# A two-layer hybrid trunk on one core: the whole body placed in a block whose instruction order comes from another scheduler model

## The chip, the cores and the metric

The kernel runs on one core of a Trainium2 chip. The time is that of the device, in microseconds (us), from the launch of the program to its end; the median of several runs is compared. The core has five engines that run their own instruction streams in order and wait for each other by semaphores: PE (TensorE, matmuls; its weight loads are shown as PEld), DVE (VectorE), ACT (ScalarE), POOL (GpSimd) and SP (SyncE, which here issues the DMAs of the weights).

## What is computed

The reference is a decoder trunk of two residual layers over 512 tokens of width 1024, float32:

```python
for i in range(DEPTH):                       # DEPTH = 2
    h = rms_norm(x, mix_norm[i])
    if i % 2 == 0:                           # layer 0
        x = x + concat([ssd_mixer(...), gla_mixer(...)]) @ w_out    # parts of h @ w_in
    else:                                    # layer 1
        x = x + mla(h)                       # latent attention, 16 heads, causal
    f = rms_norm(x, ffn_norm[i])
    x = x + (silu(f @ w_gate[i]) * (f @ w_up[i])) @ w_down[i]       # 2816 hidden
```

The SSD mixer has a causal convolution of width 4, SiLU, a chunked scan over 128 tokens, a gate `silu(z)` and an RMS norm over two groups of 512 features. The GLA mixer is a gated linear attention in chunks of 64 tokens. The attention has low-rank q and kv with norms, a rotary part and per-head norms of q and k.

## The kernel before

The residual lies feature-major in eight tiles of 128 features x 512 tokens. Every dense product runs in float32 accuracy out of three matmuls: weight and activation are each split into two parts, `hi` and `lo` (names `whi`/`wlo`, `xh`/`xl`, `mxh`/`mxl`, `fhh`/`fhl`), and `mm3` (L140 to L143) adds `hi*hi`, `lo*hi` and `hi*lo` in one PSUM bank. `weight` (L125 to L138) loads one piece of a weight, mostly 128 x 1024: a DMA on SP's queue into `wraw` (2 buffers), a cast on ACT to `whi` (L135) and a subtraction on DVE to `wlo` (L136), 3 buffers each. One such piece feeds 24 matmuls of 128 x 512. The next weight's steps are written with a raised priority (`AHEAD`, 90), so the scheduler puts them before work that the program has earlier.

Accumulators (`acc`) share three PSUM banks in turn: the fourth needs the bank of the first, so it waits for whatever reads that one. The other banks belong to roles (`st`, `a1`, `a2` in layer 0; `sco`, `ptr`, `po` in the attention).

Norms (`rstd`, L165 to L178): ones-matmuls sum the squares into `st` (L168), DVE takes the reciprocal root by a bit estimate and three Newton steps on a 128x128 tile, 12 small instructions (`rs_m`, `rsi`, `rsy`, `rst`, L156 to L161), four matmuls with `sel` spread it (L175) and ACT copies it to `R` or `Rg` (L177). The factor `R` is applied late, when a product of the layer is read out of PSUM: `xpad` (L320, input of the convolution, whose taps are `cva`, L322 and L325), `fg` and `fu` (L634, L637, gate and up of the FFN), `zh`, `kr`, `qd`. So the first products of a stage need `R` only when their bank has to come free.

Stages: the mixer with its convolution, SSD groups g = 0 and 1 (their outputs `y`, normed by `Rg` at L426, split to `mxh`, `mxl`, and taken into the residual by `out_round`), four GLA heads with three more rounds; the FFN, 22 pairs of gate and up and then the down products; the attention: low-rank products (`lh`, `ll`, squares `lsq`, per-token factors `lry`), `project` per group of four heads (q to `qs` through `acc`, k and v to `ks` and `v`, evicted with the factor `lry`; per-head sums `st` by reduces at L799 to L802, roots `hry`, then `qs` and `ks` scaled, L807 to L814, and rotated, L732 to L735), `prepare` (transposes of `ks` and `qs` to `kT` and `qT`, L821 to L836, through `acc`) and `attend` (L848 to L867); a second FFN. The number behind a name here and below is that of the buffer.

What sets the order: the program text gives instructions priorities in the order written (weights raised), and a scheduler at compile time orders each engine's stream by these priorities and by a model of when each instruction could run. The streams are then fixed; on the chip each engine takes its next instruction and waits if that isn't ready.

Of the kernel before, what the change touches and what calls it, by code (L numbers as in the profile page):

```python
# [15 lines left out]
DRAM = bass.MemoryType.DRAM  # L16
# [15 lines left out]
# columns of the packed per-partition vectors  # L32
# [11 lines left out]

@with_exitstack
def kernel(ctx: ExitStack, tc: tile.TileContext, A, yT, stop=99):
# [20 lines left out]
    def open_phase(**tags):  # L67
        """the other banks, by role"""
        if phase:
            phase["pool"].__exit__(None, None, None)  # L70
        phase["pool"] = tc.tile_pool(name=nm("pph"), bufs=1, space=PSUM)
        phase["p"] = phase["pool"].__enter__()
        phase["tags"] = tags
# [26 lines left out]
    # sel[:, c]: row 32 c is one  # L100
# [4 lines left out]
    # tri[s, l] = 1 where s <= l  # L105
# [10 lines left out]
    def split(raw_ap, th, tl, bufs, pool):  # L116
        """raw float32 [128, 512] -> exact parts hi + lo, both float32r"""
        hi = pool.tile([P, T], F32R, tag=th, name=nm(th), bufs=bufs)
        lo = pool.tile([P, T], F32R, tag=tl, name=nm(tl), bufs=bufs)
        S.copy(hi, raw_ap)  # L120
        V.tensor_tensor(lo, raw_ap, hi.bitcast(F32), ALU.subtract)
        return hi, lo

    def weight(src, kc, m):
        """src: DRAM AP [128, kc, m]; loaded and split ahead of what comes before it here"""  # L125
        with tc.high_priority(offset=AHEAD):
            return weight_now(src, kc, m)
# [17 lines left out]
    def dense(ps, w, xs):  # L145
        """ps[m, t] = sum over the chunks of w (stationary) and xs [(hi, lo)]"""
        n = len(xs)
        for k, (xh, xl) in enumerate(xs):
            mm3(ps, w[0][:, k, :], w[1][:, k, :], xh, xl, k == 0, k == n - 1)

    def rsqrt(pool, m, shape, tag, ytag=""):
        """1/sqrt(m) by bit estimate and three Newton steps; m > 0"""
        h = pool.tile(shape, I32, tag=tag + "i", name=nm(tag + "i"), bufs=1)
        y = pool.tile(shape, F32, tag=tag + ytag + "y", name=nm(tag + "y"), bufs=1)
        t = pool.tile(shape, F32, tag=tag + "t", name=nm(tag + "t"), bufs=1)
        V.tensor_scalar(h, m.bitcast(I32), 1, None, ALU.logical_shift_right)  # L156
        V.tensor_scalar(y.bitcast(I32), h, -1.0, float(0x5F3759DF), ALU.mult, ALU.add)
        for _ in range(3):
            V.tensor_tensor(t, y, y, ALU.mult)
            V.scalar_tensor_tensor(t, m, -0.5, t, ALU.mult, ALU.mult)  # L160
            V.scalar_tensor_tensor(y, t, 1.5, y, ALU.add, ALU.mult)  # L161
        return y

    def rstd(ssq, n, pool, tag):
        """ssq [128, 512]: partial sums of squares -> R [128, 512], 1/rms on every partition"""  # L165
        ps = aux()
        for c in range(4):
            E.matmul(ps[32 * c:32 * c + 32, :P], ones, ssq[:, c * P:(c + 1) * P],  # L168
                     start=True, stop=True)
        m = const.tile([P, P], F32, tag="rs_m", name=nm("rs_m"))  # L170
        V.tensor_scalar(m, ps[:, :P], 1.0 / n, EPS, ALU.mult, ALU.add)
        y = rsqrt(const, m, [P, P], "rs")
        pb = aux()
        for c in range(4):
            E.matmul(pb[:, c * P:(c + 1) * P], sel[:, c, :], y, start=True, stop=True)  # L175
        R = pool.tile([P, T], F32, tag=tag, name=nm(tag), bufs=1)
        S.copy(R, pb)  # L177
        return R  # L178

    class Norm:  # L180
        """collects the chunks of the residual: squares, and x * gain in two parts"""
# [26 lines left out]
    def tok_scalar(R):  # L208
        """R [128, 512] with equal rows -> [128 tokens, 4]"""
        ps = aux()  # L210
        for c in range(4):
            E.transpose(ps[:, c * P:(c + 1) * P], R[:, c * P:(c + 1) * P], ident)
        r = const.tile([P, 4], F32, tag="rtok", name=nm("rtok"))
        V.tensor_copy(r, ps.rearrange("p (c x) -> p c x", c=4)[:, :, 0])
        return r

    def gate(pool, tag, ps, R, bufs):
        """silu(ps * R)"""
        h = pool.tile([P, T], F32, tag="cva", name=nm(tag + "h"), bufs=2)
        V.scalar_tensor_tensor(h, ps, 0.5, R, ALU.mult, ALU.mult)  # L220
        t = pool.tile([P, T], F32, tag="cvt", name=nm(tag + "t"), bufs=2)
        S.activation(t, h, AF.Tanh)
        g = pool.tile([P, T], F32, tag=tag, name=nm(tag), bufs=bufs)
        V.scalar_tensor_tensor(g, t, 1.0, h, ALU.add, ALU.mult)
        return g

# [8 lines left out]
    def out_round(r, parts, nxt=None):  # L235
        """residual += (4 chunks of the mixed width) @ their rows of w_out"""
        for m2 in range(4):
            w = weight(A["w_out"][r, m2], 4, 256)
            for j in range(2):
                m = 2 * m2 + j  # L240
                ps = acc()
                dense(ps, (w[0][:, :, j * P:(j + 1) * P], w[1][:, :, j * P:(j + 1) * P]), parts)
                V.tensor_tensor(X[m], X[m], ps, ALU.add)
                if nxt is not None:
                    nxt.add(m)
# [8 lines left out]
    with tc.tile_pool(name="gkp", bufs=1) as gkp:  # L254
        rtok = tok_scalar(R)
        # dt (rows 0..15) and the low-rank gate input (rows 32..47)
# [9 lines left out]
        # dt = softplus(dt_raw + bias), token-major [128, chunk, head]  # L266
# [41 lines left out]
        with tc.tile_pool(name="ssd", bufs=2) as sp:  # L308
# [4 lines left out]
            def conv(i, tag, bufs, bank=acc):  # L313
                """silu(causal conv) of chunk i of x|B|C, feature-major"""
# [18 lines left out]
            def group(g):  # L333
                """B and C of a group: cb[s, l] for s <= l, C feature-major, B token-major"""
# [23 lines left out]
            def core(f, xs, zg, cb, cT, btok):  # L358
                """the scan of two heads, gated by silu(z)"""
# [8 lines left out]
                # decay times cb, [s, head, chunk, l]  # L368
# [8 lines left out]
                # exp(a_cum) on the features' partitions  # L377
# [3 lines left out]
                # x * dt, token-major; and that times the decay to the chunk's end  # L381
# [10 lines left out]
                # states at the chunk starts  # L392
# [39 lines left out]
            def values(h):  # L432
                """v of a GLA head, token-major"""
# [36 lines left out]
        with tc.tile_pool(name="gla", bufs=2) as gp:  # L470
# [5 lines left out]
            # log-sigmoid of the gates, summed inside chunks of 64  # L476
# [19 lines left out]
            def inner(h, after_dense=None):  # L496
                """normalised head output times its gain; two chunks of 128 values"""
# [3 lines left out]
                # exp(g_last / 16) of each chunk  # L501
# [12 lines left out]
                # queries of a pair's second chunk, decayed from the pair's start  # L514
# [29 lines left out]
                # scores, transposed: [key, pair, query]  # L544
# [12 lines left out]
                # keys at the pairs' ends, token-major, and the states  # L557
# [109 lines left out]
    with tc.tile_pool(name="mla", bufs=2) as mp, tc.tile_pool(name="mla1", bufs=1) as m1:  # L667
        r1 = tok_scalar(R)
        # tables with the gains: rope(x) = x * ra + swapped x * rb, for q and for k
# [12 lines left out]
        # causal mask: zeros, then -1e30 where key > query in the last block  # L682
# [5 lines left out]
        # rotary key, feature-major raw  # L688
# [5 lines left out]
        # low-rank q and kv: raw (without 1/rms of the residual), times their gains, in two parts;  # L694
        # per-token factors: cf = r1 / rms(r1 * raw)
# [29 lines left out]
        # rotary key: token-major norm and rotation, back to feature-major  # L725
        def rope(dst, src, tab, shape):
            """dst = src * ra + swapped src * rb; shape [128, 4, heads, 32]"""
# [40 lines left out]
        def project(g):  # L768
            """q, k (normalised, rotated) and v of four heads, token-major"""
            # q of four heads  # L770
# [11 lines left out]
            # k and v of four heads  # L782
# [12 lines left out]
            # 1/rms per head  # L795
# [21 lines left out]
        def prepare(g, hp, qs, ks, v):  # L817
            """keys and queries of two heads, feature-major"""
# [21 lines left out]
        def attend(g, hp, v, kts, qts):  # L840
            """two heads: scores, softmax, values"""
            po = aux("po")
            for b in range(4):
                n = (b + 1) * P
                pts = []
                for j in range(2):
# [4 lines left out]
                    # -scale * (scores + mask), and its minimum  # L851
# [6 lines left out]
                    # probabilities, transposed: [key, key block, query]  # L858
# [13 lines left out]
        def o_round(r, nxt=None):  # L872
            """residual += half of the heads @ their rows of w_o"""
# [31 lines left out]
def _layout(inp):  # L905
# [5 lines left out]
    def pieces(w, kc, m):  # L911
        """[K, M] -> [M / m, 128, kc, m]"""
# [10 lines left out]
    # [head, half of the chunks, 128, 4 chunks, 256]  # L923
    a["w_v"] = np.ascontiguousarray(v.reshape(2, 4, P, 4, 256).transpose(3, 0, 2, 1, 4))
    a["w_g"] = pieces(g, KD, P)
    # [round of 4 chunks, pair of column chunks, 128, 4, 256]
# [7 lines left out]
    # [group of 4 heads, 128, 3, 384]  # L934
    a["w_uq"] = pieces(i["w_uq"][0], 3, 384)
    # [group, 128, 2, (k | v) x 4 heads x 64]
# [22 lines left out]
    # rotary tables, of shapes alone: [128, (cos | sin with sign), 4, 32]  # L959
# [26 lines left out]
```

## Time and profile before

| | us |
|---|---|
| median of 3 runs (lowest, highest) | 1395.1 (1395.07, 1395.79) |
| span of the profiled execution | 1393.5 |
| PE busy | 1373.1 (99%) |
| DVE busy | 786.1 (56%) |
| ACT busy | 559.6 (40%) |

The profile has one execution of the kernel. Its span goes from the first to the last recorded instruction, and lies 1.6 us under the median of the timed runs. A row of the timeline has start and duration in us, engine, line of the kernel, operation, output and inputs; in square brackets the idle time ahead of it and what ended that. A row of a stretch (`0.00:50.00`) has its length, then for each engine the busy time and in brackets the number of instructions, the clock granted to TensorE (1.00 is full), and the use of the DMAs. A row of waits has who waited for whom, the total, how often, and the longest. A row of groups has line, engine, operation, the tiles with their shape, count, then busy time and the mean of one in ns, then the idle time of the engine just before them and what ended it. Matmul records overlap: one of 128 x 512 is shown for 0.39 us, and the next starts 0.23 us after it.

### The profile page before, as it was taken

The numbers are of one execution on the slowest core, as the hardware profiler recorded it, in microseconds if no ns is written. First come the engines' busy times: TensorE is split into PE (matmuls) and PEld (weight loads), VectorE is DVE, ScalarE is ACT, GpSimd is POOL, SyncE is SP. The second block draws the span as 40 slices with busy tenths as digits, with TensorE's granted clock in tenths as the row PEclk, the third lists the DMA queues.
The fourth block names the chain that finished last, engine by engine and source line by source line (L and its number), as shares of the span: only waits on it lengthen the run. The fifth ranks groups of instructions, "written<-read, shape, count | busy, mean of one in ns | idle before, by whom it ended". The sixth has DMA issues, their size and how long they took to land.

```text
span 1393.5 us, 17395 instructions
## 1 busy us (share of the span) xinstructions
PE 1373.1 (99%) x6842; PEld 1108.1 (80%) x6842; DVE 786.1 (56%) x1407; ACT 559.6 (40%) x934; POOL 9.1 (1%) x40
## 2 busy tenths in 40 slices
PE   7999999999999999999999998999999999999998
PEld 5798888687788888888888787767688888888887
DVE  7877956767667444444333459776684444443221
ACT  5665623544334232232232247774753323232111
POOL 0000000000000000000000000000000000000000
PEclk9999999999999999999999999999999999999999
DMA  5343232212233333333333321102023333333331
GB/s 174 108 148 94 68 99 77 65 57 76 65 102 91 93 104 92 105 91 94 92 101 96 99 68 49 44 31 76 1 76 106 91 103 93 92 105 102 105 109 64
DMA packets 36722, 122.21 MB, mean 88 GB/s; under 512 B 4737, under 2 KB 5761, under 8 KB 36641
## 3 DMA queue, kind: packets, MB, share of 16 engines
q1 hardware_dynamic: 35600, 120.70, 28.7%
q8 instruction: 54, 0.88, 0.3%
q10 hardware_dynamic: 1040, 0.41, 0.1%
q14 instruction: 28, 0.22, 0.1%
HBM read 118.96 MB, written 2.13 MB: 87 GB/s over the span
## 4 chain that ended last, share of the span: by engine, by line
PE 94%; DVE 4%; DMA 1%; issue 1%; ACT 1%; SPq 0%; DVEq 0%; ACTq 0%
PE acc L142 27%; PE acc L143 27%; PE acc L141 27%; PE sco L848 3%; PE po L867 2%; PE ptr L861 2%; PE st L175 1%; PE a L409 1%; DVE wlo L136 1%; PE a L579 1%; PE a L395 0%; DMA acb<-acd 0%; PE a L581 0%; PE a L413 0%; PE a L142 0%
## 5 line engine op out<-in xcount | busy, mean ns | idle before, releaser
L135 ACT CAST whi<-wraw 128x1024 fp32r<-128x1024 f32 (+2 forms) x223 | 226.6, 1017 | 576.8 <-PE acc L142 519.5
L143 PE MATMUL acc<-xh,wlo 128*128 128x512 f32 (+1 forms) x1152 | 452.5, 393 | 0.0
L142 PE MATMUL acc<-xl,whi 128*128 128x512 f32 (+1 forms) x1152 | 451.9, 392 | 0.0
L141 PE MATMUL acc<-xh,whi 128*128 128x512 f32 (+1 forms) x1152 | 451.0, 392 | 0.0
L136 DVE TENSOR_TENSOR wlo<-wraw,whi 128x1024 fp32r<-128x1024 f32 (+2 forms) x223 | 263.0, 1180 | 177.0 <-ACT whi L135 176.1
L142 PEld LDWEIGHTS acc<-xl,whi 128*128 128x128 f32 (+1 forms) x1152 | 215.7, 187 | 47.3 <-issue 3.1
L143 PEld LDWEIGHTS acc<-xh,wlo 128*128 128x128 f32 (+1 forms) x1152 | 215.7, 187 | 45.8 <-issue 1.8
L141 PEld LDWEIGHTS acc<-xh,whi 128*128 128x128 f32 (+1 forms) x1152 | 215.8, 187 | 45.1 <-issue 1.1
L141 PE MATMUL acc<-fhh,whi 128*128 128x512 f32 x288 | 112.0, 389 | 0.0
L142 PE MATMUL acc<-fhl,whi 128*128 128x512 f32 x288 | 112.0, 389 | 0.0
L143 PE MATMUL acc<-fhh,wlo 128*128 128x512 f32 x288 | 112.0, 389 | 0.0
L637 DVE TENSOR_TENSOR fu<-acc,R 128x512 f32<-128x512 f32 x44 | 30.4, 691 | 139.4 <-PE acc L143 139.4
L634 DVE TENSOR_TENSOR fg<-acc,R 128x512 f32<-128x512 f32 x44 | 30.4, 691 | 95.2 <-PE acc L143 91.3
L142 PEld LDWEIGHTS acc<-fhl,whi 128*128 128x128 f32 x288 | 54.1, 188 | 11.3
L143 PEld LDWEIGHTS acc<-fhh,wlo 128*128 128x128 f32 x288 | 54.1, 188 | 11.2
L141 PEld LDWEIGHTS acc<-fhh,whi 128*128 128x128 f32 x288 | 54.1, 188 | 11.1
L141 PE MATMUL acc<-mxh,whi 128*128 128x512 f32 x128 | 50.4, 396 | 1.3 <-ACT whi L135 1.3
L142 PE MATMUL acc<-mxl,whi 128*128 128x512 f32 x128 | 50.4, 395 | 0.0
L143 PE MATMUL acc<-mxh,wlo 128*128 128x512 f32 x128 | 50.3, 394 | 0.0
L848 PE MATMUL sco<-kT,qT 96*128 96x128 f32 (+3 forms) x128 | 45.4, 448 | 0.9 <-DVE mx L852 0.7
L852 DVE CUSTOM_DVE_ANT_0 sc<-sco,am 128x128 f32<-128x128 f32 (+3 forms) x64 | 30.8, 485 | 13.0 <-PE sco L848 12.4
L854 ACT ACTIVATE sc<-sc,mx 128x128 f32<-128x128 f32 (+3 forms) x64 | 35.8, 561 | 3.8 <-DVE mx L852 2.8
(290 smaller groups left out, 1590.6 us busy)
## 6 DMA issues: line engine op xcount, KB each, us to landing
wraw<-in_w_gate_dram SPq DMA_DIRECT2D x44, 512.0 KB, 3.6
wraw<-in_w_up_dram SPq DMA_DIRECT2D x44, 512.0 KB, 3.6
wraw<-in_w_down_dram SPq DMA_DIRECT2D x32, 512.0 KB, 3.6
wraw<-in_w_out_dram SPq DMA_DIRECT2D x16, 512.0 KB, 3.7
wraw<-in_w_xbc_dram SPq DMA_DIRECT2D x12, 512.0 KB, 3.7
wraw<-in_w_down_dram SPq DMA_DIRECT2D x16, 384.0 KB, 3.1
wraw<-in_w_z_dram SPq DMA_DIRECT2D x8, 512.0 KB, 3.6
wraw<-in_w_v_dram SPq DMA_DIRECT2D x8, 512.0 KB, 3.7
```

What stands on the lines that cost most here:

```text
L135: S.copy(hi[:, :kc * m], r)
L136: V.tensor_tensor(lo[:, :kc * m], r, hi.bitcast(F32)[:, :kc * m], ALU.subtract)
L141: E.matmul(out, ah, bh, start=first, stop=False)
L142: E.matmul(out, ah, bl, start=False, stop=False)
L143: E.matmul(out, al, bh, start=False, stop=last)
L634: V.tensor_tensor(g, pg, R, ALU.mult)
L637: V.tensor_tensor(u, pu, R, ALU.mult)
L848: E.matmul(ps[:, :n], qts[j][:, b * P:(b + 1) * P], kts[j][:, :n], start=True, stop=True)
L852: V.tensor_tensor_reduce(sc[:, :n], ps[:, :n], am[:, T - n:], -scale, 3e38, ALU.add, ALU.min, mx[:, 0:1])
L854: S.activation(sc[:, :n], sc[:, :n], AF.Exp, bias=mx[:, 0:1], scale=-1.0, accum_out=mx[:, 1:2])
L861: E.transpose(ps[:, kb * P:(kb + 1) * P], sc[:, kb * P:(kb + 1) * P], ident)
L867: E.matmul(po[64 * j:64 * j + 64, b * P:(b + 1) * P], v[:, kb, 2 * hp + j, :], pts[j][:, kb * P:(kb + 1) * P], start=(kb == 0), stop=(kb = ...
```

## The change

The body, until now `tile_trunk_kernel`, becomes a function `trunk`, and `tile_trunk_kernel` opens a block on the tile context around its call. The block is ordered with a timeline model of the engines in place of the scheduler's usual one. No operation, tile, buffer count or priority changes; comments and docstrings go, and lines in the body move down by 5.

```diff
+def tile_trunk_kernel(tc: tile.TileContext, A, yT):
+    with tc.block(name="trunk", schedule_with_timeline_sim=True):
+        trunk(tc, A, yT)
+
+
 @with_exitstack
-def tile_trunk_kernel(ctx: ExitStack, tc: tile.TileContext, A, yT, stop=99):
+def trunk(ctx: ExitStack, tc: tile.TileContext, A, yT, stop=99):
     nc = tc.nc
     V, S, G, E = nc.vector, nc.scalar, nc.gpsimd, nc.tensor
```

All five streams hold the same instructions in another order. Of PE's 6288, 3558 stand at the same place, of DVE's 1409, 454, of ACT's 880, 342, of SP's 250, 231, of POOL's 45, 31. In both FFNs the order is the same apart from their first 20 us; the mixer, the attention and the joints between stages differ.

DVE near the start, the instructions up to `xpad_66`, which takes the accumulator `acc_65` out of its bank (`cva` are the taps of the convolution, `dr`, `db`, `dp` the small chain of the time step, `bT` the activated B). Before:

```order
L280 TENSOR_TENSOR db_255<-da_252 128x64
L330 SCALAR_TENSOR_TENSOR bT_49_338<-cvt_48_336,cva_47_331 128x512
L282 TENSOR_SCALAR dp_260<-db_255 128x64
L325 SCALAR_TENSOR_TENSOR cva_55_374<-xpad_54_371,cw_295,cva_55_374 128x512
L284 SCALAR_TENSOR_TENSOR dp_260<-dp_260,db_255 128x64
L320 TENSOR_TENSOR xpad_66_427<-acc_65_402,R_32_193 128x512
```

And now:

```order
L219 COPY rtok_34_207<-st_33_202 128x4
L330 SCALAR_TENSOR_TENSOR cva_47_332<-xpad_46_329,cw_296,cva_47_332 128x512
L330 SCALAR_TENSOR_TENSOR cva_55_375<-xpad_54_372,cw_296,cva_55_375 128x512
L141 TENSOR_TENSOR wlo_130_726<-wraw_128_723,whi_129_725 128x1024
L276 TENSOR_TENSOR dr_251<-st_39_246,dtb_242 128x64
L325 TENSOR_TENSOR xpad_66_428<-acc_65_403,R_32_194 128x512
L325 TENSOR_TENSOR xpad_95_569<-acc_94_544,R_32_194 128x512
```

The weight part `wlo_130` now stands ahead of `xpad_66`, right behind the last taps of `cva_47` and `cva_55`; of the small chain of the time step, which was mixed in with the taps, only `dr` is still ahead of it. The weight part `wlo_122`, which came after `xpad_66`, stands just above these rows, ahead of `dg`.

PE at the norm of the second SSD group (`st_384` spreads the root; `acc_428` is the first product of the `out_round` behind it, with the normed `y` as `mxh` and `mxl`). Before:

```order
L142 MATMUL acc_403_2303<-wlo_399_2221,xh_14_139 128x256
L175 MATMUL st_384_2185<-rsy_382_2172,sel_97 128x128 x4
L143 MATMUL acc_403_2303<-whi_398_2220,xl_15_140 128x256
L141 MATMUL acc_403_2303<-whi_398_2220,xh_17_146 128x256
L142 MATMUL acc_403_2303<-wlo_399_2221,xh_17_146 128x256
L143 MATMUL acc_403_2303<-whi_398_2220,xl_18_147 128x256
```

And now:

```order
L147 MATMUL acc_419_2415<-xl_24_162,whi_417_2411 128x512
L148 MATMUL acc_419_2415<-xh_23_161,wlo_418_2412 128x512
L180 MATMUL st_384_2186<-rsy_382_2173,sel_98 128x128 x4
L146 MATMUL acc_428_2459<-mxh_386_2194,whi_426_2455 128x512
L147 MATMUL acc_428_2459<-mxl_387_2195,whi_426_2455 128x512
L148 MATMUL acc_428_2459<-mxh_386_2194,wlo_427_2456 128x512
L146 MATMUL acc_428_2459<-mxh_388_2199,whi_426_2455 128x512
```

Before, `st_384` stood within `acc_403`, and 60 rows of other matmuls lay between it and `acc_428`; now it stands behind the whole of `acc_419`, and `acc_428` follows it at once.

DVE at the start of the attention, from the scaling of `ks_1171` to the last step of the rotation of `qs_1157`, which PE then transposes (`st_1205` and `sq_1204` belong to the second group of heads, `qs_1157` to the first). Before:

```order
L814 TENSOR_TENSOR ks_1171_6670<-ks_1171_6670,hry_1180_6719 128x1024
L732 TENSOR_TENSOR rt_1183_6735<-rr_1182_6733,csq_6271 128x16x16
L733 TENSOR_TENSOR rt_1183_6735<-rr_1182_6733,csq_6271 128x16x16
L734 TENSOR_TENSOR qs_1157_6607<-rr_1182_6733,csq_6271 128x16x32
L799 TENSOR_REDUCE st_1205_6843<-sq_1204_6842 128x16
L735 TENSOR_TENSOR qs_1157_6607<-qs_1157_6607,rt_1183_6735 128x16x32
L800 TENSOR_REDUCE st_1205_6843<-sq_1204_6842 128x16
```

And now:

```order
L819 TENSOR_TENSOR ks_1171_6671<-ks_1171_6671,hry_1180_6720 128x1024
L804 TENSOR_REDUCE st_1205_6844<-sq_1204_6843 128x16
L805 TENSOR_REDUCE st_1205_6844<-sq_1204_6843 128x16
L737 TENSOR_TENSOR rt_1183_6736<-rr_1182_6734,csq_6272 128x16x16
L738 TENSOR_TENSOR rt_1183_6736<-rr_1182_6734,csq_6272 128x16x16
L739 TENSOR_TENSOR qs_1157_6608<-rr_1182_6734,csq_6272 128x16x32
L809 TENSOR_SCALAR st_1205_6844<-st_1205_6844 128x16
L141 TENSOR_TENSOR wlo_1277_7111<-wraw_1275_7108,whi_1276_7110 128x1024
L809 TENSOR_SCALAR st_1205_6844<-st_1205_6844 128x16
L835 TENSOR_SCALAR kT1_6598<-acc_1211_6876,pv_89 64x512
L807 TENSOR_REDUCE st_1205_6844<-sq_1204_6843 128x16
L740 TENSOR_TENSOR qs_1157_6608<-qs_1157_6608,rt_1183_6736 128x16x32
```

The reduce of 512 columns, the weight part `wlo_1277`, the copy `kT1` and the third reduce now stand ahead of the last step of `qs_1157`; so do `wlo_1267` and `wlo_1270`, which stood behind it before and are now further up among the roots `hry_1180`.

More of the change, by code (lines that the diff above doesn't have):

```diff
@@ L42, with kernel @@
 NPV = _n
+def kernel(tc: tile.TileContext, A, yT):
+    with tc.block(name="trunk", schedule_with_timeline_sim=True):
+        trunk(tc, A, yT)
 @with_exitstack
-def kernel(ctx: ExitStack, tc: tile.TileContext, A, yT, stop=99):
+def trunk(ctx: ExitStack, tc: tile.TileContext, A, yT, stop=99):
     nc = tc.nc
```

## The prediction

> **What bounds the kernel now.** I read the page first: how busy each engine is, and the chain that ended last.
>
> ```profile
> span 1393.5 us, 17395 instructions
> PE 1373.1 (99%) x6842; PEld 1108.1 (80%) x6842; DVE 786.1 (56%) x1407; ACT 559.6 (40%) x934; POOL 9.1 (1%) x40
> PE 94%; DVE 4%; DMA 1%; issue 1%; ACT 1%; SPq 0%; DVEq 0%; ACTq 0%
> ```
>
> TensorE (PE) is the bound, and an order without any operation added or removed can change the time only by making PE stand still more or less. So the second view is busy time by stretches: 0 to 435 us is the mixer, 435 to 800 the first FFN, 800 to 1025 the attention, the rest the second FFN.
>
> ```profile
> core 0: us, PE busy (x) PEld busy (x) DVE busy (x) ACT busy (x) POOL busy (x), PEclk, DMA share, GB/s
> 0.00:50.00 50.00, 42.41 (x198) 30.84 (x199) 38.77 (x76) 25.34 (x39) 3.20 (x22) 1.00 0.39 133
> 250.00:300.00 50.00, 46.89 (x259) 36.82 (x257) 35.02 (x58) 22.89 (x35) 0.00 (x0) 0.97 0.22 64
> 450.00:500.00 50.00, 50.00 (x222) 41.42 (x221) 23.48 (x29) 15.12 (x19) 0.00 (x0) 1.00 0.34 98
> 850.00:900.00 50.00, 46.26 (x278) 34.03 (x276) 41.66 (x129) 37.80 (x87) 0.00 (x0) 1.00 0.14 44
> 900.00:950.00 50.00, 49.15 (x296) 32.06 (x295) 36.87 (x125) 36.37 (x93) 0.00 (x0) 1.00 0.14 43
> ```
>
> In an FFN (450 to 500) PE never idles: 222 matmuls in 50 us, one each 0.225 us. PE stands still 7 us at the start, 3 us in 250 to 300, and 3.7 us in 850 to 900, where DVE is busy 83% of the time. The third view, PE's waits, names them:
>
> ```profile
> PE a L141 <- ACT xh L193: 6.9, 1, 6.9
> PE a L548 <- DVE ki L529: 1.6, 1, 1.6
> PE acc L834 <- DVE qs L735: 1.4, 1, 1.4
> PE acc L141 <- ACT whi L135: 1.3, 1, 1.3
> PE acc L834 <- DVE kT L830: 1.0, 1, 1.0
> PE acc L821 <- ACT qT L836: 0.7, 2, 0.6
> ```
>
> The first is the load of the input, which no order moves. So what the old order visibly loses is about 8 us. A new order has little to win that shows, and every place where it lets PE run into an unfinished result is a loss. A dense matmul's record lasts 0.39 us while the next starts 0.225 us later, so waits under 0.165 us at hand-overs stay hidden; there are some 200 hand-overs between dense and small matmuls in mixer and attention, so at most 33 us could hide there.
>
> **The change part by part.** Nothing is added or removed; instructions of each engine change places. Both FFN bodies keep their order. SP's queue keeps 231 of 250 places, and a weight lands 3.6 us after its issue (row below) against a weight's 5.4 us of matmuls (24 of 0.225); I cost it at nothing. The terms are the places where PE now meets a result just made, worked out with the durations of these groups:
>
> ```profile
> L135 ACT CAST whi<-wraw 128x1024 fp32r<-128x1024 f32 x197 | 207.0, 1051 | 516.2 <-PE acc L142 468.3 <-issue 33.8 <-PE acc L143 7.8
> L136 DVE TENSOR_TENSOR wlo<-wraw,whi 128x1024 fp32r<-128x1024 f32 x197 | 240.6, 1222 | 171.0 <-ACT whi L135 170.1 <-PE st L168 0.7
> L325 DVE SCALAR_TENSOR_TENSOR cva<-xpad,cw,cva 128x512 f32<-128x512 f32 x36 | 26.7, 742 | 0.2
> L320 DVE TENSOR_TENSOR xpad<-acc,R 128x512 f32<-128x512 f32 x10 | 6.9, 686 | 0.5 <-PE acc L143 0.5
> L634 DVE TENSOR_TENSOR fg<-acc,R 128x512 f32<-128x512 f32 x44 | 30.4, 691 | 95.2 <-PE acc L143 91.3 <-ACT R L177 3.9
> L799 DVE TENSOR_REDUCE st<-sq 128x16 f32<-128x1024 f32 x4 | 4.9, 1214 | 2.5 <-ACT sq L798 2.5
> wraw<-in_w_gate_dram SPq DMA_DIRECT2D x44, 512.0 KB, 3.6
> 229.47 0.59 ACT L177 COPY Rg<-st 128x512 f32<-128x512 f32 x1 [0.45 <-PE st L175]
> ```
>
> *T1, the start.* `acc_102` is the fourth user of three accumulator banks: it must wait for `xpad_66`, which reads `acc_65`. The new DVE order puts much ahead of `xpad_66`. Counting from the start of `st_31`: ACT casts `whi_121` first (1.05), then copies R (1.64); DVE does `wlo_122` (2.3), `dg` and two `xpad` (4.4), six `cva` (8.9), `rtok`, `wlo_130` (10.3), `dr` (10.6), `xpad_66` (11.3). PE has until then only `st_31` (0.9), 24 matmuls of `acc_94` (5.4) and eight small ones (0.8): it stands from 7.1 to 11.3, **+4.2**.
>
> *T2, norm of the second SSD group, then `out_round`.* The rows of before for the same chain:
>
> ```profile
> 228.30 1.13 PE L175 MATMUL st<-rsy,sel 128*128 128x128 f32 x8 [0.18 <-DVE rsy L161]
> 230.19 2.73 DVE L426 SCALAR_TENSOR_TENSOR y<-y,pv,Rg 128x512 f32<-128x512 f32 x4
> 231.97 2.18 ACT L120 CAST mxh<-y 128x512 fp32r<-128x512 f32 x4
> 232.84 1.89 DVE L121 TENSOR_TENSOR mxl<-y,mxh 128x512 fp32r<-128x512 f32 x3
> 243.92 0.39 PE L141 MATMUL acc<-mxh,whi 128*128 128x512 f32 x1
> ```
>
> From `st` to the first `mxl` written are 5.2 us (228.30 to 232.84, and 0.68 for one), and PE came for it only at 243.92: hidden. In the new order the dense matmuls stand right behind `st_384`, with `whi_436` and `wlo_437` in the chain: 1.05 + 0.59 + 0.6 (the rest of `wlo`) + 2.73 + 0.7 = 5.7, less 1.1 of PE's own work, **+4.6**.
>
> *T3, both FFN starts.* `acc_743` waits for `fg_732`, as `acc_727` holds its bank. New order: from `st_722` on ACT casts `whi_753` (1.05) ahead of R, DVE does `wlo_754` (to 2.3) ahead of `fg` (3.0); PE has 0.9 of work: 2.1 each, **+4.2**.
>
> *T4, attention start.* Three places. (a) `acc_1176` needs the bank of `acc_1173`, whose eviction needs `lry_1149`. In before that chain took 4.3 us:
>
> ```profile
> 829.23 0.16 DVE L718 SCALAR_TENSOR_TENSOR lm<-sco,rtok 128x4 f32<-128x4 f32 x1 [1.21 <-PE sco L716]
> 833.34 0.15 DVE L722 TENSOR_TENSOR lry<-lry,rtok 128x4 f32<-128x4 f32 x1
> 850.84 0.68 DVE L735 TENSOR_TENSOR qs<-qs,rt 128x512 f32<-128x512 f32 x1
> 851.44 0.68 DVE L800 TENSOR_REDUCE st<-sq 128x16 f32<-128x512 f32 x1
> 851.67 1.05 PE L834 MATMUL acc<-ident,qs 128*96 128x128 f32 x8 [1.41 <-DVE qs L735]
> 854.77 0.75 DVE L830 TENSOR_SCALAR kT<-acc,pv 64x512 f32<-64x512 f32 x1
> ```
>
> Now two reduces (1.21 + 0.68) stand in it and it begins later: some 6.1, plus two evictions 0.7, less 2.7 of matmuls: 4.1. (b) Ahead of the last `qs` that `acc_1212` transposes there are now two more `wlo` (128x768 and 128x384, together 1.4 by their share of the 1.22 of a full one), a reduce of 0.68, a `wlo` of 1.22, `kT` 0.75 and a reduce of 1.21: 5.3 more than in before, where PE already waited 1.4: 6.7. (c) `acc_1271` waits for the bank of `acc_1216`, read by `kT3`, which stands behind the next group's rsqrt and three scalings: 2.8. Together 13.6, less what this stretch waited before (1.4 + 1.0 + 0.7), **+10.5**.
>
> *T5, the clock.* A long stop costs twice. Before, after the 1.62 and 1.29 us near 264, matmuls started 0.43 apart for 3.2 us:
>
> ```profile
> 262.00:264.00 2.00, 0.94 (x5) 0.44 (x3) 2.00 (x4) 0.06 (x1) 0.00 (x0) 1.00 0.02 8
> 264.00:266.00 2.00, 0.34 (x4) 0.20 (x4) 2.00 (x5) 1.80 (x3) 0.00 (x0) 0.92 0.02 4
> 266.00:268.00 2.00, 1.81 (x4) 1.49 (x5) 2.00 (x5) 0.76 (x3) 0.00 (x0) 0.50 0.04 8
> 268.00:270.00 2.00, 2.00 (x8) 1.60 (x7) 1.32 (x2) 0.81 (x2) 0.00 (x0) 0.72 0.00 0
> ```
>
> At a granted 0.50 that is 1.6 us lost. I count it after T1, T2 and once in T4, **+4.8**. The Trainium skill ("TensorE: Matmul & The Clock Gate", section "HAM oscillation — how this bites in real kernels") says to leave PE no idle gap over about 3.4 us, as the clock then falls to half for a window; by it T4 would pay twice and the sum would be 1.6 higher. The trace agrees that a stretch with little PE work is followed by about 3.2 us at half clock.
>
> *Gains.* The stop near 264 goes: `ki` is made well ahead there now. 1.6 + 1.3 + 1.6 of clock, **−4.5**. PE changes from dense to small matmuls 86 times instead of 97; I take 0.1 each, **−1.1**. Small hidden waits: of the PE instructions that use a DVE or ACT result, 404 stood under 2 us of PE work behind its producer by my count of the listing, and 123 do now. Worth between 0 and the 33 us above; I take **−10**, near a third, since where DVE is 83% busy a wait moves on rather than goes.
>
> Sum: 4.2 + 4.6 + 4.2 + 10.5 + 4.8 − 4.5 − 1.1 − 10 = +12.7 on 1393.5, so a span of 1406.2. The median of the runs shown, 1395.1, lies 1.6 over the profiled span: **1407.8 us**.
>
> **The rivals.**
> 1. *Faster.* The hidden waits are worth twice as much (18), and DVE, given idle stretches by PE's stops, comes to T4 (b) and (c) early, so that T4 costs 3 and its clock penalty goes: 28.3 − 7.5 − 1.6 − 23.6 = −4.4, 1390.7 us. The point is whether DVE is behind when `acc_1212` comes. For it: DVE is busy 56% overall. Against: 83% where it matters.
> 2. *No change.* T3 and T4 at half, without T4's clock penalty (4.2 + 4.6 + 2.1 + 5.3 + 3.2 = 19.4), against hidden waits of 14 (19.6 with the other gains): 1394.9 us. That the block orders nothing is excluded: the orders differ.
> 3. *Much slower.* DVE's backlog of T4 lasts through the attention, and each of the next scalings (1.2 us, twice a group) is waited for; no hidden wait is won. 12.7 + 10 + 1.6 for a second clock penalty = +24.3, 1419.4 us. For it: DVE at 83% in 850 to 900. Against: by 900 to 950 it is at 74%.
>
> **How the numbers follow.** Forecast (1398 to 1414): 0.50; much slower: 0.18; no change: 0.12; faster: 0.20. Halving T1 to T4 gives 1396; no gain from hidden waits 1417.8. The range, 1390 to 1420, takes in rival 1's time and rival 3's. Within 0.2% (2.8 us, about what a measurement here can tell from none): 0.12, as the case has it; slower 0.68, faster 0.20.
>
> **What would show it.** In the new profile: a PE wait of about 4 us before `acc` near 47 us, on DVE `xpad`; one of about 4.5 on `mxl` or `mxh` at the `out_round` near 240; a 2 us wait at each FFN start on `fg`; 4, 7 and 3 us in 830 to 880 on `ks`/`v`, `qs` and `kT`, with a granted clock under 1 behind the long ones; no wait on `ki`. Wrong it would be if PE's busy time in 0 to 50 and 850 to 900 does not fall, or if waits that add to 20 us appear while the span falls (hidden waits worth more than I took).

## The result and the profile after

| | before | after |
|---|---|---|
| median, us (4 runs each) | 1395.44 (1395.07 to 1396.37) | 1406.0 (1402.97 to 1406.65) |
| ratio after / before | | 1.0072 (95% interval 1.0059 to 1.0084) |
| span of the profiled execution | 1393.5 | 1404.6 |

The changed kernel is slower by 0.7%: 11.1 us between the two profiled executions, where +12.7 was forecast; 1407.8 was named, 1406.0 measured. The profiled execution of the changed kernel is the slowest of its four runs (1406.65); the fastest took 3.7 us less.

The engines' row on the page of the changed kernel:

```profile
PE 1371.2 (98%) x6842; PEld 1117.1 (80%) x6842; DVE 788.1 (56%) x1407; ACT 560.7 (40%) x934; POOL 10.0 (1%) x40
```

The work is the same; PE stands more, and in places its clock is lower. Its waits in the changed kernel (who waited for whom: total, times, longest):

```profile
PE a L146 <- ACT xh L198: 6.8, 1, 6.8
PE acc L839 <- DVE st L809: 6.3, 1, 6.3
PE acc L146 <- DVE fg L639: 3.8, 2, 1.9
PE acc L146 <- DVE xpad L325: 2.8, 1, 2.8
PE acc L146 <- ACT v L799: 2.6, 1, 2.6
PE acc L146 <- ACT mxh L125: 2.4, 1, 2.4
PE acc L826 <- DVE ks L819: 1.7, 1, 1.7
PE acc L147 <- DVE mxl L126: 1.4, 1, 1.4
PE acc L146 <- ACT xh L125: 0.7, 1, 0.7
PE st L274 <- DVE rtok L219: 0.4, 1, 0.4
```

Below the load of the input, which both kernels have, these and one more of 0.4 come to 22.5 us; in before the listed waits were 8.4. So 14.1 us of visible waits came in. They are at the places named: `xpad` (start), `mxh`/`mxl` (the `out_round`), `fg` (both FFN starts, twice 1.9), and `v`, `ks` and the last step of `qs` (attention start; the row names `st` at L809, a small DVE instruction that ended at 865.24, but what the transposes read is `qs`, whose last step ended just before it, at 865.15; PE went on at 865.30). The wait on `ki` is gone.

The stretches that answer to those of before, then short ones behind the stops (length, busy time of PE, PEld, DVE, ACT, POOL with instructions, granted clock, DMA):

```profile
0.00:50.00 50.00, 39.94 (x172) 29.30 (x173) 32.10 (x54) 24.31 (x36) 3.08 (x21) 0.97 0.47 150
250.00:300.00 50.00, 50.00 (x205) 37.65 (x205) 31.00 (x40) 21.36 (x27) 1.49 (x4) 0.98 0.21 65
850.00:900.00 50.00, 42.01 (x227) 33.32 (x225) 43.03 (x122) 37.34 (x81) 3.82 (x5) 0.90 0.16 55
900.00:950.00 50.00, 50.00 (x320) 36.33 (x320) 40.17 (x125) 37.18 (x93) 0.00 (x0) 1.00 0.10 32
48.00:54.00 6.00, 5.81 (x14) 4.61 (x15) 5.92 (x16) 1.54 (x4) 0.10 (x1) 0.52 0.31 87
246.00:252.00 6.00, 4.21 (x10) 3.17 (x11) 5.34 (x9) 2.16 (x4) 1.49 (x4) 0.72 0.29 91
448.00:452.00 4.00, 3.94 (x17) 3.29 (x18) 2.47 (x5) 3.06 (x4) 0.00 (x0) 1.00 0.42 131
866.00:870.00 4.00, 4.00 (x23) 3.89 (x21) 3.72 (x11) 2.74 (x5) 0.00 (x0) 0.56 0.00 0
```

PE is busy 2.5 us less in 0 to 50 and 4.3 less in 850 to 900, and 3.1 more in 250 to 300. Behind the stops at the start, the `out_round` and the attention start the clock is near half; behind the 1.9 us stop of the FFN (448 to 452) it is not. In 48 to 54, 14 matmuls kept PE busy for 5.8 us; at 0.227 us each, the distance of their starts at full clock, they are 3.2 us of work. So 2.6 us went to the clock there alone.

### The profile page after: what moved, and what is told of

Same layout as the page of the kernel before. It is cut to its first block, busy times and chain, and to the rows that moved or that the text cites. A ratio compares the mean times of both kernels' runs of the same rounds, so it can differ in the third digit from the quotient of the medians.

```text
span 1404.6 us, 17383 instructions
## 1 busy us (share of the span) xinstructions
PE 1371.2 (98%) x6842; PEld 1117.1 (80%) x6842; DVE 788.1 (56%) x1407; ACT 560.7 (40%) x934; POOL 10.0 (1%) x40
## 4 chain that ended last, share of the span: by engine, by line
PE 96%; DVE 3%; ACT 1%; DMA 0%; issue 0%; SPq 0%; ACTq 0%; DVEq 0%
PE acc L147 28%; PE acc L146 27%; PE acc L148 27%; PE sco L853 3%; PE po L872 2%; PE ptr L866 2%; PE acc L839 1%; PE a L414 1%; DVE wlo L141 1%; PE a L584 1%; PE a L147 0%; PE st L180 0%; PE a L148 0%; PE a L146 0%; PE a L573 0%; PE a L586 0%
## 5 line engine op out<-in xcount | busy, mean ns | idle before, releaser
L146 PEld LDWEIGHTS acc<-fhh,whi 128*128 128x128 f32 x288 | 54.1, 188 | 11.3
L859 ACT ACTIVATE sc<-sc,mx 128x128 f32<-128x128 f32 (+3 forms) x64 | 36.0, 563 | 10.8 <-DVE mx L857 10.6
```

What stands on the lines that cost most here:

```text
L146: E.matmul(out, ah, bh, start=first, stop=False)
L859: S.activation(sc[:, :n], sc[:, :n], AF.Exp, bias=mx[:, 0:1], scale=-1.0, accum_out=mx[:, 1:2])
```

## The experiments

All hold back instructions ("pin" them) by `tc.issue_after(i)`: what the program writes inside it comes behind `i` on `i`'s engine, as an order, without a wait. Work, tiles and buffers stay as they are. `pin` is a dictionary of the instructions to stay behind. "Cover" is other work that PE has between making one result and needing the next. The block without the flag and without pins was not run; `old_all2` below has the block without the flag, and its stop near 264 us is the one of before.

A pin also shifts what the scheduler does later. So beside the whole time stand two marks of each profile, from the views of the tiles `fg` and `krr` (start of the first `fg`, and of `krr`, the first result of the attention), and what is left from `krr` to the end of the span. The marks are of one execution each, and hold what the clock cost in that one:

| kernel | median, us (lowest to highest) | first fg | krr | krr to end |
|---|---|---|---|---|
| before | 1395.44 (1395.07 to 1396.37) | 438.9 | 796.4 | 597.1 |
| after | 1406.0 (1402.97 to 1406.65) | 447.3 | 799.0 | 605.6 |
| pin_start | 1399.54 (1398.87 to 1402.98) | 442.6 | 794.2 | 603.6 |
| pin_out | 1395.83 (1394.2 to 1397.74) | 441.3 | 794.5 | 598.3 |
| pin_ffn | 1399.78 (1398.27 to 1401.38) | 446.3 | 798.0 | 599.4 |
| pin_ffn2 | 1398.69 (1396.92 to 1400.3) | 444.2 | 795.8 | 601.0 |
| pin_att | 1396.63 (1395.51 to 1398.68) | 447.2 | 798.8 | 597.1 |
| pin_so | 1395.03 (1391.33 to 1399.04) | 439.8 | 791.4 | 602.9 |
| pin_all2 | 1384.05 (1383.22 to 1385.06) | 436.4 | 788.1 | 594.2 |
| old_all2 | 1396.6 (1394.55 to 1397.86) | 439.5 | 796.9 | 598.4 |

The kernel before, run beside the experiments, had medians of 1394.89 (first four) and 1395.12 (last four).

### pin_start: two weights behind `xpad_66`

```diff
-                w = weight(A["w_xbc"][i], KD, P)
+                with ExitStack() as late:
+                    if i == 2:
+                        late.enter_context(tc.issue_after(pin["R"].ins))
+                        late.enter_context(tc.issue_after(pin["xpad"].ins))
+                    w = weight(A["w_xbc"][i], KD, P)
```

The same for `w_z` at f = 2; `pin["xpad"]` is the `xpad` of i = 0.

> The changed kernel, with two weights of the mixer's start (whi/wlo 122 and 130) pinned behind the copy of R on ACT and behind xpad_66 on DVE. Theory (the stop ahead of acc_102 is what stands ahead of xpad_66 on DVE): the 2.8 us wait of acc on xpad falls to under 0.7 us and the half-clock stretch behind it (0.52 from 48 to 54 us, some 2.2 us lost) goes, so 1401.5 to 1403 us against 1406.0. Rival (PE would stand there anyway, for the next bank or weight): the wait changes its name, the time stays within 1405 to 1407.

Waits of PE in this kernel, and the clock behind:

```profile
PE acc L147 <- DVE xpad L330: 0.8, 1, 0.8
48.00:54.00 6.00, 6.00 (x28) 4.97 (x27) 6.00 (x14) 2.39 (x4) 0.00 (x0) 1.00 0.59 178
```

2.8 falls to 0.8, a little above the 0.7 expected, and the clock is 1.00 with 28 matmuls instead of 14 in the same 6 us. `krr` comes 4.8 us earlier. The whole time, 6.5 below the changed kernel, is under the expected 1401.5 to 1403: from `krr` on it is 2.0 shorter as well, where nothing was pinned. The long waits there are the same (2.6, 1.7 and 6.3); what is gone is the half clock behind the 2.6, which took 1.7 in the changed kernel (by the distances of its matmuls from 841 to 846). The theory holds at its place for the wait, and the rival is out. That the shorter wait saved the clock is not shown: `pin_so` below has the same pins and the same 0.8 wait, and this clock:

```profile
48.00:54.00 6.00, 6.00 (x23) 4.86 (x22) 5.25 (x12) 1.69 (x4) 0.00 (x0) 0.81 0.58 175
```

### pin_out: cover between `st_384` and `acc_428` again

```diff
+                with ExitStack() as late:
+                    if h == 0:
+                        late.enter_context(tc.issue_after(pin["ones"].ins))
+                    dense(ps, w, xp)             # w_q
...
+                with ExitStack() as late:
+                    if h == 0:
+                        late.enter_context(tc.issue_after(pin["sel"].ins))
+                    dense(ps, w, xp)             # w_k
```

`pin["ones"]` and `pin["sel"]` are the last matmuls of the latest `rstd`, here `st_379` and `st_384`.

> The changed kernel, with the q product of the first GLA head pinned on PE behind the squares' sum st_379 and its k product behind st_384, so that 24 dense matmuls (5.4 us) stand between st_384 and acc_428 again. Theory (missing cover): the waits of acc on mxh and mxl (2.4 and 1.4 us) fall under 0.5 us together, and the clock stays 1.00 in 246 to 252 us (0.72 now): 1400.5 to 1402.5 us against 1406.0. Rival (the cover is taken from another place, which then stands): a new wait of PE of 3 us or more ahead of st_379, st_384 or later in the head, 1404.5 to 1407.

Two of its waits, and its clock at that place:

```profile
PE acc L846 <- DVE st L816: 3.8, 1, 3.8
PE st L174 <- DVE ysq L469: 1.6, 1, 1.6
248.00:254.00 6.00, 6.00 (x26) 4.72 (x26) 2.95 (x4) 1.74 (x2) 0.00 (x0) 1.00 0.15 58
```

The waits on `mxh` and `mxl` are not in the list any more, the clock is 1.00, and of 3.8 us a new wait of 1.6 on `ysq` comes back ahead of `st_379`, a smaller form of what the rival said. `krr` is 4.4 earlier. The whole time is far below both expectations, because from `krr` on it is 7.3 shorter with nothing pinned there: the wait for `qs` fell from 6.3 to 3.8, the one for `ks` (1.7) is gone, and the clock is 1.00 throughout, although the 2.6 us wait on `v` is still there. So the size of the `qs` wait is an accident of the order that the scheduler arrives at, not a fixed cost of the flag.

### pin_ffn: the weights of the FFN behind `R` and `fg`

```diff
+                with ExitStack() as late:
+                    if c == 2:
+                        late.enter_context(tc.issue_after(pin["R"].ins))
+                        late.enter_context(tc.issue_after(pin["fg"].ins))
+                    w = weight(A["w_up"][layer, c], KD, P)
```

The same for `w_gate`.

> The changed kernel, with the two weights of the third pair of each FFN pinned behind the copy of R on ACT and the first fg on DVE. Theory (the 1.9 us wait at each FFN start is fg kept back by a weight's cast and subtraction): both waits of acc on fg vanish or fall under 0.3 us, 1401 to 1402.5 us against 1406.0. Rival (the pinned weights come late and acc_751 waits for them instead): a wait on whi or wlo of 1 to 2 us at each FFN start, 1404.5 to 1407.

```profile
PE acc L147 <- DVE fg L648: 3.2, 2, 1.8
PE acc L850 <- DVE st L820: 2.5, 1, 2.5
```

A miss: with no weight ahead of `fg`, the two waits are still 1.8 and 1.4 (row 1, twice together 3.2). Neither theory nor rival is met at the place, and the first `fg` comes only 1.0 us earlier; the whole time, under both ranges, fell through the attention (row 2: 6.3 to 2.5). The rows of the changed kernel at the first FFN say why:

```profile
438.02 0.43 PE L173 MATMUL st<-sq,ones 128*32 128x128 f32 x8
445.09 1.05 PE L180 MATMUL st<-rsy,sel 128*128 128x128 f32 x8
447.32 0.68 DVE L639 TENSOR_TENSOR fg<-acc,R 128x512 f32<-128x512 f32 x1
448.06 0.50 PE L146 MATMUL acc<-xh,whi 128*128 128x512 f32 x1 [1.92 <-DVE fg L639]
```

From the sum of squares (`st`, 438.02) to the matmuls that spread the root are 7.1 us. PE has by 438.02 done 43 of the 72 matmuls of the first three products, and the other 29 fill those 7.1 us; when it reaches the second `st` all three banks are full, and R (0.59) and `fg` (0.68) lie bare behind it: nothing is left for PE to do meanwhile.

### pin_ffn2: keep the cover for the sum

```diff
                 pu = acc()
-                dense(pu, w, xp)
+                with ExitStack() as late:
+                    if c == 0:
+                        late.enter_context(tc.issue_after(pin["ones"].ins))
+                    dense(pu, w, xp)
```

> The changed kernel, with the up product of each FFN's first pair pinned on PE behind the squares' sum (st_717, st_1714), so that the first gate product alone stands ahead of it; the weights are left where the scheduler puts them. Theory now (the FFN-start wait on fg comes from PE having spent the cover, two products of 5.4 us, before the sum, so that sel matmuls, R and fg lie bare): both waits on fg fall under 0.4 us each, the first FFN's body begins 1.5 to 2 us earlier than in the changed kernel. Rival (pin_ffn's: the weight parts on ACT and DVE hold fg back): the waits stay at 1.4 us or more. The attention's order shifts as well with any pin, so the whole time is not the test: 1397 to 1404 us by both.

```profile
PE acc L147 <- DVE fg L643: 0.6, 2, 0.3
```

0.3 each, with the weights left where the scheduler put them. The first `fg` comes 3.1 us earlier, where 1.5 to 2 was expected, but 1.5 of this was there already at the `out_round` near 246, ahead of all that was pinned, most of it through less half clock at the start; the pin's share is 1.6. The cause of the stop is the spent cover.

### pin_att: DVE's order ahead of the first transposes

```diff
+            with ExitStack() as late:
+                if g == 0:
+                    late.enter_context(tc.issue_after(pin["cf"].ins))
+                elif g == 1:
+                    late.enter_context(tc.issue_after(pin["rope", 0].ins))
                 V.tensor_reduce(st[:, 0], sq[:, :, 0:64], AX.X, ALU.add)
                 V.tensor_reduce(st[:, 1], sq[:, :, 64:96], AX.X, ALU.add)
```

The weights of `project(2)` and the one `kT` copy of the first two heads that is DVE's (`kT1`) go behind `pin["rope", 0]`, the last step of the first group's rotation, too; `pin["cf"]` is the last step of `lry` for kv.

> The changed kernel, with project's first reduces pinned on DVE behind the kv factor lry, and the second group's reduces, the third group's weights and the first kT copies behind the last step of the first group's rotation of qs. Theory (DVE's order ahead of the first transposes is the largest loss): the waits of acc on ks, v and st/qs at 840 to 866 us (2.6, 1.7 and 6.3 us, 10.6 together) fall to 4 us or less together, and half-clock time there to under 1 us: 1397 to 1400.5 us against 1406.0. Rival (DVE is simply behind at this stage: 43 of 50 us busy in 850 to 900, so the wait moves to the second group): waits on qs, kT or sc of 5 us or more later in the attention, 1403.5 to 1407.

```profile
PE acc L854 <- DVE kT L850: 1.0, 1, 1.0
PE acc L147 <- ACT v L806: 1.0, 1, 1.0
PE acc L854 <- DVE qs L741: 0.9, 1, 0.9
```

10.6 us of waits became 2.9, with no half clock in the attention, and from `krr` to the end are 597.1, as in before: 8.5 less than in the changed kernel. No later wait took their place, so the rival is out. The median, 1396.63, is 0.4 under the theory's range (1397 to 1400.5). The pins moved reduces, weights and a copy together, so the share of each is open.

### pin_so, pin_all2 and old_all2: together, and with the usual model

`pin_so` has the pins of pin_start and pin_out; `pin_all2` adds pin_att and pin_ffn2; `old_all2` is `pin_all2` without the flag:

```diff
-    with tc.block(name="trunk", schedule_with_timeline_sim=True):
+    with tc.block(name="trunk"):
```

> The changed kernel with the pins of pin_start and of pin_out together. Theory (the two stops are independent, local losses of the mixer): the first attention product (krr) comes 8.5 to 9.5 us earlier than in the changed kernel (4.8 and 4.4 for each alone), so near 790 us, ahead of the kernel before (796.4) by some 6.5; whole time 1389 to 1394 us if the attention's order is that of pin_out. Rival (one backlog of DVE that both pins work off): 5 to 6 us, krr at 793 to 794.

> The changed kernel with the pins of pin_start, pin_out, pin_att and pin_ffn2. Theory (the new order is better than the old one except at its joints): 1406.0 less 4.8, 4.4, 10.2 and 3.5 for the two FFN starts: 1381 to 1386 us, below the kernel before by 9 to 13 us. Rival (what the pins give back is only what the new order lost, and stops move): 1390 to 1395 us, no better than before.

> The same pins with the scheduler's usual model (the block without the flag). Theory (the gain under the stops is the new model's: fewer short waits and no ki wait): the pins do little here, since the old order has none of these stops but the attention's start (4.3 us): 1389 to 1396 us, and pin_all2 is faster than it by 5 us or more. Rival (it is the pins that make a good order, whatever the model): within 3 us of pin_all2.

`pin_so`: `krr` at 791.4 is 7.6 earlier than in the changed kernel, between theory (8.5 to 9.5) and rival (5 to 6). The missing 1 to 2 us need no common backlog: the half clock at the start, shown above, took some 1.7 in this execution and nothing in that of `pin_start`. Its median missed the range by 1 us, and five of its twelve runs (1391.33 to 1393.76) lie within it; its attention kept a longer wait than that of `pin_out` (3.8):

```profile
PE acc L856 <- DVE qs L757: 5.2, 1, 5.2
```

The largest waits of `pin_all2` behind the load, and then of `old_all2`:

```profile
PE st L174 <- DVE ysq L479: 1.6, 1, 1.6
PE acc L873 <- DVE kT L869: 1.0, 1, 1.0
PE acc L147 <- ACT v L825: 1.0, 1, 1.0
PE acc L147 <- DVE fg L659: 0.9, 2, 0.7
```

```profile
PE acc L857 <- ACT qT L875: 2.5, 2, 2.3
PE a L570 <- DVE ki L551: 1.6, 1, 1.6
PE acc L147 <- ACT whi L141: 1.3, 1, 1.3
```

`pin_all2` is 22 us under the changed kernel, within its theory's range, and faster than the kernel before: ratio 0.9924 (0.9911 to 0.9937). `old_all2` has the same pins and the old model: 1.0014 (1.0005 to 1.0023) of the kernel before, 0.6 us over its range, with the `ki` and `whi` waits of before still in it. So the pins are worth nothing in the old order and 22 us in the new one, and the new order without its stops is worth 12.5 us by the medians (13.0 by the profiles: `krr` 8.8 us earlier in `pin_all2`, the rest 4.2 behind it). The rival for `pin_all2` (no better than before) and the one for `old_all2` (within 3 us of it) are out.

Where do the 13.0 come from? Beside the load, the listed waits of the two are the same: 8.3 us in `old_all2`, 8.6 in `pin_all2`. `old_all2` has two stretches at half clock (266 to 271 and 854 to 858), worth some 3 us; `pin_all2` has none until its last microseconds. So some 10 us of the gain (an estimate: what is left) is in no listed wait.

## Why the prediction was right

Term by term, in us of the profiled execution:

| term | put | measured |
|---|---|---|
| T1, start | +4.2 | +3.2 (2.8, and 0.4 on `rtok`) |
| T2, `out_round` | +4.6 | +3.8 (2.4 + 1.4) |
| T3, two FFN starts | +4.2 | +3.8 |
| T4, attention start | +10.5 (13.6 − 3.1) | +7.5 (2.6 + 1.7 + 6.3 − 3.1) |
| waits of `ki` and `whi` | −2.9 | −2.9 |
| other listed waits | none | −1.3 |
| clock, net of the 1.6 in before | +3.2 | some +6 (estimate) |
| hand-overs and hidden waits | −11.1 | some −9 (what is left) |
| sum | +12.7 | +11.1 |

*Right in kind.* Each forecast stop but T4's (c) is there, on the tile named and with the engine named, and the experiments took the stops at T1, T2 and T4 away, or most of them, by the order blamed for them. The listed waits rose by 14.1 where 20.6 was put; the clock cost some 3 us more than put, and the hidden gains are some 2 smaller. These errors go against each other, so it is luck that the sum came within 1.6 us. Which run was profiled is luck too: the four of the changed kernel differ by 3.7 us, and the one on which the column rests is the slowest.

*T1* was summed 0.8 too long, and PE got there 0.6 later. The rows (`st`, R, `xpad`, then the matmul):

```profile
37.67 1.05 PE L180 MATMUL st<-rsy,sel 128*128 128x128 f32 x8
38.76 0.59 ACT L182 COPY R<-st 128x512 f32<-128x512 f32 x1
42.09 2.78 DVE L330 SCALAR_TENSOR_TENSOR cva<-xpad,cw,cva 128x512 f32<-128x512 f32 x4 [0.37 <-ACT cva L327]
48.19 0.79 PE L146 MATMUL acc<-xh,whi 128*128 128x512 f32 x1 [2.77 <-DVE xpad L325]
```

The chain to the matmul took 10.5 us, not 11.3: instructions of DVE one behind the other overlap by some 0.05 each (four taps in 2.78, not 4 x 0.742). And PE arrived later since it waited 0.4 for `rtok` on the way, and the eight small matmuls between 43.6 and 45.4 cost it some 0.3 more than the 0.8 put.

*T2* was put at 4.6 and measured 3.8. The missing cover is shown by `pin_out`; what `whi_436` and `wlo_437` in the chain add was not tested apart.

*T3* had the right size for a partly wrong reason. Its step "ACT casts `whi_753` ahead of R, DVE does `wlo_754` ahead of `fg`" is worth 0.5 us at the first start and 0.1 at the second (pin_ffn: 1.4 and 1.8 left). What decides is that PE spent its three banks before the sum of squares was in (pin_ffn2: 0.3 left).

*T4* is the term that was mis-sized. (a) was put at 4.1 and measured 2.6. (b) was put at 6.7 for `qs` and measured 6.3, with 1.7 for `ks` ahead of it, which was not put. (a) and (b) together were put at 10.8 and measured 10.6: what PE did not wait for `v` it waited for `ks` and `qs`, as one would expect where DVE sets the pace (no run tests it). (c), 2.8 for the bank of `acc_1216`, did not come. The rows of the changed kernel:

```profile
852.73 3.82 POOL L767 COPY kT<-kT 32x512 f32<-32x512 f32 x5 [60.65 <-ACT kT L765]
853.43 0.52 DVE L165 SCALAR_TENSOR_TENSOR hrt<-st,hrt 128x48 f32<-128x48 f32 x1
854.54 1.53 DVE L812 TENSOR_TENSOR qs<-qs,hry 128x1024 f32<-128x1024 f32 x1
856.00 1.09 DVE L815 TENSOR_TENSOR rr<-qs,hry 128x512 f32<-128x512 f32 x1
865.30 1.91 PE L839 MATMUL acc<-ident,qs 128*96 128x128 f32 x8 [6.30 <-DVE st L809]
869.93 0.42 PE L146 MATMUL acc<-whi,lh 128*128 128x384 f32 x1
870.90 0.76 DVE L835 TENSOR_SCALAR kT<-acc,pv 64x512 f32<-64x512 f32 x1
```

The last two rows show (c): the dense product began (869.93) before that `kT` copy had read its bank (870.90), so it did not wait for this bank as the prediction had it; which bank it got the rows don't say. In (b) the five copies of POOL fell on DVE's chain to `qs` and stretched its rows by some 1.7 us (the last section has them). That hardly adds to the difference: in before the same copies fell on the roots `hry` of this chain, and stretched rows by some 1.5.

*The clock* cost more than put. Three places were counted at 1.6 each, and four were slow. By the distances of the dense matmuls, 2.7 us went behind T1, 1.7 at the `out_round` and 1.7 behind the wait on `v`; behind the wait on `qs`, where PE has small matmuls, some 1.5 (estimate, against the same transposes in `pin_out`). The Trainium skill ("TensorE: Matmul & The Clock Gate", section "HAM oscillation — how this bites in real kernels") draws the line at an idle gap of about 3.4 us. Here the length of a gap did not decide it. A wait of 2.77 us was enough, and one of 1.92 at the first FFN start was not (448 to 452: 1.00); but the same 1.9 us was followed by half clock in `pin_out`:

```profile
444.00:446.00 2.00, 2.00 (x6) 1.57 (x5) 1.31 (x2) 1.09 (x2) 0.00 (x0) 0.50 0.16 66
```

The waits of 2.6 and 3.8 in the attention of `pin_out` were not followed by it, and in `pin_so` one of 0.8 behind one of 0.6 was. So the price of a stop in clock, put here as a fixed 1.6, came out between nothing and 2.7, and no run here shows what sets it.

*Hidden waits*: −10 was taken between 0 and −33; with the switches, some −9 is left over for both. `pin_all2` against `old_all2` gives a second figure for the same thing, the 10 us that are in no listed wait. The two agree, but both are remainders: no run shows a single hidden wait, nor that their count (404 against 123) sets the gain.

One slip in the prediction changed nothing here: rival 1 doubles the hidden waits to 18, where twice the 10 put is 20, and with 20 its time would be 1388.7 us.

## What to carry to other kernels

A new order can be better in most places and still slower as a whole: here the other scheduler model was worth 12.5 us between the joints of the stages and lost 22 at five of them, and only the sum showed up in the time. Read at each joint what stands ahead of the one instruction that frees a bank or ends a norm, and count the cover in PE time behind the last matmul of that chain; here a handful of pins at these joints was enough. And where any pin reshuffles a later stage, judge it by marks at the stage borders, by the wait it was meant for and by the clock of that execution, not by the whole time alone.

## What was not expected of the hardware

While POOL copied `kT`, DVE was slower. In the rows above, an instruction of 128x48 took 0.52 us instead of 0.21, the scaling of `qs` 1.53 and the one of `rr` 1.09. In before, where the same copies came earlier, these two took:

```profile
845.56 1.23 DVE L807 TENSOR_TENSOR qs<-qs,hry 128x1024 f32<-128x1024 f32 x1
846.71 0.68 DVE L810 TENSOR_TENSOR rr<-qs,hry 128x512 f32<-128x512 f32 x1
840.69 2.84 POOL L762 COPY kT<-kT 32x512 f32<-32x512 f32 x5 [51.61 <-ACT kT L760]
```

In before, the copies ran beside small DVE instructions of the roots; there it was these that were slow (0.62 to 0.53 us instead of 0.21 or less). The copies took 3.82 us instead of 2.84 as well. The Trainium skill ("SBUF — State Buffer", section "Who interferes with whom") says that DVE and GpSimd share a pair of ports, and that a `tensor_tensor` with both inputs in SBUF contends with GpSimd's reads; the traces agree for these two. No run moved the copies alone, but where pins moved them the slow rows moved too: in `pin_out` they start at 843.00, and the scaling of `qs` at 846.93, behind them, took 1.22 us and that of `rr` 0.68; in `pin_ffn` they start at 847.98, and the two, beside them, took 1.54 and 1.09.

The time of a kernel with stops goes with its clock from run to run. The four runs of the changed kernel took 1402.97 us at a mean granted clock of 0.995 and 1405.46 to 1406.65 at 0.991 to 0.993. The twelve of `pin_so` went from 1391.33 at 0.999 to 1399.04 at 0.993, 7.7 us apart. `pin_all2`, without the long stops, spreads 1.8 us in five runs, at 0.998 to 1.000. The kernel before has a spread of 1.3 in the four runs of the table above, but of 3.4 in the 23 beside the last experiments, so it isn't shown that the changed kernel spreads more than it.
